# A two-layer encoder on one core: mixer tokens in column order, mixer B's products 160 wide, and all its heads turned by VectorE and GpSimd

## The chip, the cores and the metric

The kernel runs on one core of a Trainium2 chip. The metric is the device time of one execution in microseconds, as the median of several runs. The engines are TensorE (PE in the profile, its weight loads PEld), VectorE (DVE), ScalarE (ACT), GpSimd (POOL) and SyncE (SP), which issues the DMAs. Each engine works through its own list of instructions in order and waits on semaphores for what it needs from the others.

## The reference

An encoder of two layers over 256 tokens with 2048 features, all in float32. Each layer has a sub-layer of two mixers side by side and a feed-forward sub-layer; the shift, scale and gate of each come from one linear map of `c` ("ada"). Cut to what matters here:

```python
h = rmsnorm(x, norm_mix[l]) * (1.0 + sc_a) + sh_a
qa, ka, va, qb, kb, vb, ga, gb = split_cols(h @ w_in[l])
ya = window_attention(qa, ka, va, sink_a[l]) @ w_proj_a[l]        # 8 heads, |i-j| <= 128
yb = neighbourhood_attention(qb, kb, vb, rel_bias_b[l]) @ w_proj_b[l]  # 8 heads
merged = jax.nn.sigmoid(ga) * ya + jax.nn.sigmoid(gb) * yb
x = x + gt_a * (merged @ w_out[l])
h = rmsnorm(x, norm_ffn[l]) * (1.0 + sc_m) + sh_m
u = depthwise_conv(h @ w_up[l], conv_w[l], conv_b[l])
g, v = jnp.split(u, 2, axis=-1)
x = x + gt_m * ((jax.nn.silu(g) * v) @ w_down[l])
```

The 256 tokens of mixer B are a grid of 4 rows by 64 columns, token = row * 64 + column. A token attends to all 4 rows (`NA_KH` is 8, clamped to 4) and to a window of 16 columns around its own, with a learned bias by the offset; all other scores are -1e30 before the softmax.

## The kernel before

Activations lie with features on partitions and 256 tokens along a row. All weights are streamed once, in the order of use, as units of 16 blocks of 128x128: a DMA of 1 MB on SP into a tile `w` (four buffers, shared with the ada tiles `aw`), then in two halves ScalarE casts the block to a rounded fp32r high part and VectorE subtracts for the low part (`hl`, lines 326 and 327). TensorE makes three products for each block, high times high, high times low and low times high (lines 343 to 345 with 256 columns; lines 406 to 408 with 512 columns, where the weights move and the tokens are stationary: that is how q, k, v come out with tokens on partitions). The ada map is a row reduction on VectorE (line 233, 2.35 us for each of 189 tiles of 1 MB).

Everything else is fitted between the units. `Stream.tick` runs after each unit and lets background jobs go on; one of them is `attention()`, a generator in which each live head takes one step at a time: its start (for mixer B with the load of its bias into `p`, line 880), scores and softmax, for some heads the turn of the probabilities, their split into high and low parts (`pT`), and the product with v (`po`, line 689). A scheduler in the framework then settles the order on each engine; on SP it is the order of issue. SP's DMAs take eight landing semaphores in turn (DMAHW0 to DMAHW7), and a DMA waits until the one that had its semaphore before has landed.

The pieces that the change touches:

- `normed` (line 494) writes the modulated norm `ht` on VectorE (line 497), from which ScalarE and VectorE make the high and low parts of h, for both sub-layers (`w` is 0 for the mixers).
- `small(l)` loads the tables: maskA (128x512), cs (the rotary table, 128x64), gains, rg, sink and cw, one DMA each (line 178).
- `attend` makes a head's scores as two products of 256 keys for 128 queries each. In layer 0 these are plain float32 (two passes on TensorE for one product), in layer 1 three fp32r products each (`SCORES_3`). The reduction at line 654 adds mask or bias and takes the maximum, ScalarE makes the exponentials and the scaling (lines 662 and 670).
- The turn: in layer 0, four transposes of 128x128 on TensorE into `tp` (line 681). In layer 1, VectorE transposes blocks of 32x32 (line 304) and GpSimd puts the blocks in their places with 16 copies of 32x128 (line 298). `MOVED = [(0,0), (8,8)]` says how many heads of mixers A and B in each layer are turned in this second way. ScalarE and VectorE then write `pT` (lines 418 and 421) and TensorE makes po with six products of 256 columns.
- In the gates and the merge, mixer A's branch `ya` is multiplied by its gate, mixer B's by `gb`, and `merge` adds both on VectorE (line 1014) and splits the sum for `w_out`.

Of the kernel before, what the change touches and what calls it, by code (L numbers as in the profile page):

```python
# [30 lines left out]
BLOCK = 32  # L31

# [57 lines left out]
MOVED = [(0,0), (8,8)]  # L90
# [51 lines left out]
def encoder(ctx: ExitStack, tc: tile.TileContext, a: dict, out: bass.AP):  # L142
# [45 lines left out]
    sp = pool("s", 1)  # L188

# [118 lines left out]

    def unit_steps(l, u, by_halves=False):
# [181 lines left out]
    def normed(l, w, h, rbs):  # L491

        mod, amod = mods[l], amods[l]
        for kc in range(KC):
            t = ev.tile([P, S], F32, name="ht", tag="z")
            sh = mod[:, 3 * w * KC + kc : 3 * w * KC + kc + 1]
            nc.vector.scalar_tensor_tensor(
                out=t[:], in0=x[:, kc], scalar=amod[:, w, kc : kc + 1], in1=rbs[:], op0=ALU.mult, op1=ALU.mult
# [147 lines left out]
    def attend(q, k, v, p, mask, scale, sink, o, rows=None):  # L646

        sc = ax.tile([P, 2, S], F32, name="sc", tag="ax")
        for t in range(2):
            for i, j in by(q):  # L650
                nc.tensor.matmul(sc[:, t], q[i][:, t * P : (t + 1) * P], k[j], start=i + j == 0, stop=(i, j) == by(q)[-1])  # L651
        m = sm.tile([P, 2], F32, name="m", tag="m")
        for t in range(2):
            nc.vector.tensor_tensor_reduce(
                out=p[:, t], in0=sc[:, t], in1=mask[:, t], scale=scale, scalar=-3.0e38 if sink is None else sink,
                op0=ALU.add, op1=ALU.max, accum_out=m[:, t : t + 1],
            )
# [3 lines left out]
        for t in range(2):  # L661
            nc.scalar.activation(out=p[:, t], in_=p[:, t], func=AF.Exp, bias=nm[:, t : t + 1], accum_out=den[:, t : t + 1])
# [6 lines left out]
        for t in range(2):  # L669
            nc.scalar.activation(out=p[:, t], in_=p[:, t], func=AF.Copy, scale=ri[:, t : t + 1])  # L670
        yield
        if rows is not None:
            turned_blocks(p[:], rows(), 2)
            for _ in range(STEPS[sink is None]):
                yield
            tp = p
        else:
# [5 lines left out]
        split(pT, tp[:], held=rows is not None)  # L683
# [124 lines left out]
    for l in range(L):  # L808
# [17 lines left out]
        if l:  # L826


            def bare_gate(mo):
                def evac(ps):  # L830
                    z, sh = bare.level(ps, 0.5)
                    half_tanh(ya[:, mo], z[:], bias=sh[:, :1])
# [17 lines left out]
        def head_a(i):  # L850
# [18 lines left out]
            def rows():  # L869
# [3 lines left out]
                q, k, v, p, tables[0], SCALE, sink[:, i : i + 1], lambda: oA[i], rows if i < MOVED[l][0] else None  # L873
            )

        def head_b(hb):
# [3 lines left out]
            nc.sync.dma_start(p[:], a["bias"][l, hb])  # L880
# [323 lines left out]
```

## Time and profile before

| | us |
|---|---|
| median of 3 runs | 2653.98 |
| lowest, highest | 2653.20, 2656.04 |
| the profiled execution's own time | 2661.45 |
| its span in the trace | 2659.6 |
| TensorE busy | 2643.3 |
| VectorE busy | 2121.0 |
| ScalarE busy | 1408.9 |
| GpSimd busy | 228.2 |

A share of busy time is a mean over stages with different limits, so the page's totals only say where to look. What counts is, stage by stage, which engine is full and how long before its use each operand is there. The 40 slices of the page show TensorE at 90% or more in each slice, so a stall of TensorE is lost time wherever it falls, and work of another engine costs only where TensorE has to wait for it. Matmuls overlap in the records, so a product's price is the distance from one start to the next in the timeline, or the length of a stretch over the count, not its own duration.

The trace has the granted TensorE clock at 1.00 throughout. The DMA queues moved 700.42 MB at a mean of 263 GB/s, 371 GB/s in the first slice.

### The profile page before, as it was taken

The page shows a single profiled execution, that of the slowest core. Times are in us where ns is not written, and L with a number is a line of the kernel's source. Part 1 is how long each engine was busy: PE and PEld are TensorE (multiplying, and loading weights), DVE is VectorE, ACT ScalarE, POOL GpSimd, SP SyncE. Part 2 cuts the span into 40 slices and gives each one's busy share as a digit, 9 for nine tenths or more (in the row PEclk, how much of TensorE's full clock was granted, in tenths as well). Part 3 has the DMA queues.
Part 4 walks back from the last instruction along what each step waited for, and adds up shares of the span by engine and source line. Part 5 has one row for each costly group of instructions (what it writes and reads, how often), then busy time and mean ns, then how long its engine had stood idle before and what let it go on. Part 6 is the DMA issues. An engine that isn't in the chain of part 4 may idle for free.

```text
span 2659.6 us, 51014 instructions
## 1 busy us (share of the span) xinstructions
PE 2643.3 (99%) x21164; PEld 2557.9 (96%) x21164; DVE 2121.0 (80%) x2979; ACT 1408.9 (53%) x2280; POOL 228.2 (9%) x345
## 2 busy tenths in 40 slices
PE   9999999999999999999999999999999999999999
PEld 7888899999999999999998889999999999999999
DVE  8898998997987888788886778868888866655664
ACT  5445865456643555355554666654565445544553
POOL 0001100000000000000002558520000000000000
PEclk9999999999999999999999999999999999999999
DMA  9987779885777777877766666666747765555554
GB/s 371 349 329 292 267 294 356 316 339 184 295 272 289 284 287 285 306 296 285 283 221 253 249 234 232 253 258 257 283 178 287 297 252 191 192 196 194 196 191 143
DMA packets 102042, 700.42 MB, mean 263 GB/s; under 512 B 12721, under 2 KB 15025, under 8 KB 17969
## 3 DMA queue, kind: packets, MB, share of 16 engines
q1 hardware_dynamic: 101810, 697.17, 70.8%
q8 instruction: 165, 2.70, 0.4%
q14 instruction: 67, 0.55, 0.1%
HBM read 695.03 MB, written 2.10 MB: 262 GB/s over the span
## 4 chain that ended last, share of the span: by engine, by line
PE 86%; DMA 5%; DVE 5%; issue 2%; ACT 1%; POOL 0%; SPq 0%; DVEq 0%; ACTq 0%
PE ps L343 24%; PE ps L345 24%; PE ps L344 24%; DMA aw<-in_aw 4%; PE ps_t L408 4%; PE ps_t L407 4%; PE ps_t L406 4%; DVE hl L327 2%; DVE aw L233 1%; PE sc L651 1%; ACT hl L326 1%; PE po L689 1%; DMA w<-in_ws 1%; DVE u L1049 0%; POOL qrs L472 0%
## 5 line engine op out<-in xcount | busy, mean ns | idle before, releaser
L327 DVE TENSOR_TENSOR hl<-w,hl 128x1024 fp32r<-128x1024 f32 x928 | 1129.8, 1224 | 298.0 <-ACT hl L326 294.7
L326 ACT CAST hl<-w 128x1024 fp32r<-128x1024 f32 x928 | 969.8, 1049 | 719.7 <-PE ps L345 501.4
L343 PE MATMUL ps<-h,hl 128*128 128x256 f32 x3328 | 922.4, 277 | 1.3 <-DVE ya L970 0.6
L344 PE MATMUL ps<-h,hl 128*128 128x256 f32 x3328 | 919.6, 276 | 0.0
L345 PE MATMUL ps<-h,hl 128*128 128x256 f32 x3328 | 919.6, 277 | 0.0
L343 PEld LDWEIGHTS ps<-h,hl 128*128 128x128 f32 x3328 | 624.7, 188 | 2.4 <-DVE ya L970 0.8
L344 PEld LDWEIGHTS ps<-h,hl 128*128 128x128 f32 x3328 | 625.3, 188 | 0.4 <-DVE h L501 0.2
L345 PEld LDWEIGHTS ps<-h,hl 128*128 128x128 f32 x3328 | 624.4, 188 | 0.0
L233 DVE CUSTOM_DVE_ANT_0 aw<-aw,cact,ab 128x2048 f32<-128x2048 f32 x189 | 443.8, 2349 | 92.5 <-DMA aw<-in_aw 91.7
L406 PE MATMUL ps_t<-hl,h 128*128 128x512 f32 x576 | 223.0, 392 | 2.7 <-ACT h L500 2.0
L407 PE MATMUL ps_t<-hl,h 128*128 128x512 f32 x576 | 225.0, 391 | 0.3
L408 PE MATMUL ps_t<-hl,h 128*128 128x512 f32 x576 | 224.3, 390 | 0.0
L1049 DVE SCALAR_TENSOR_TENSOR u<-ps,cw,u 128x255 f32<-128x255 f32 x304 | 146.0, 480 | 62.0 <-ACT u L1047 58.1
L1047 ACT ACTIVATE u<-ps,cw 128x256 f32<-128x256 f32 x152 | 85.7, 564 | 155.4 <-PE ps L345 155.2
L343 PE MATMUL ps<-act_o,hl 128*128 128x256 f32 x512 | 142.0, 278 | 2.7 <-DVE u L1049 2.6
L345 PE MATMUL ps<-act_o,hl 128*128 128x256 f32 x512 | 142.1, 278 | 1.3 <-DVE hl L327 1.3
L344 PE MATMUL ps<-act_o,hl 128*128 128x256 f32 x512 | 142.0, 277 | 0.0
L345 PE MATMUL ps<-merged,hl 128*128 128x256 f32 x512 | 141.5, 277 | 0.0
L344 PE MATMUL ps<-merged,hl 128*128 128x256 f32 x512 | 141.5, 276 | 0.0
L343 PE MATMUL ps<-merged,hl 128*128 128x256 f32 x512 | 141.5, 277 | 0.0
L406 PEld LDWEIGHTS ps_t<-hl,h 128*128 128x128 f32 x576 | 107.9, 188 | 26.1 <-ACT h L500 3.0
L407 PEld LDWEIGHTS ps_t<-hl,h 128*128 128x128 f32 x576 | 108.1, 188 | 23.9 <-DVE hl L327 1.9
(244 smaller groups left out, 4800.3 us busy)
## 6 DMA issues: line engine op xcount, KB each, us to landing
w<-in_ws SPq DMA_DIRECT2D x463, 1024.0 KB, 4.9
aw<-in_aw SPq DMA_DIRECT2D x189, 1024.0 KB, 6.3
p<-in_bias SPq DMA_DIRECT2D x16, 256.0 KB, 4.5
x<-in_xT SPq DMA_DIRECT2D x4, 512.0 KB, 5.5
aw_o<-in_aw SPq DMA_DIRECT2D x2, 1024.0 KB, 12.4
out<-x SPq DMA_DIRECT2D x16, 128.0 KB, 3.2
w<-in_ws SPq DMA_DIRECT2D x2, 512.0 KB, 11.8
aw_b<-in_aw SPq DMA_DIRECT2D x1, 1024.0 KB, 18.1
```

Of the source, the lines that this page charges most:

```text
L233: nc.vector.tensor_tensor_reduce(out=raw[:], in0=raw[:], in1=cact[:], scale=1.0, scalar=ab[:, i : i + 1], op0=ALU.mult, op1=ALU.add, accum ...
L326: nc.scalar.copy(hl[:, 0], r)
L327: nc.vector.tensor_tensor(out=hl[:, 1], in0=r, in1=hl[:, 0].bitcast(F32), op=ALU.subtract)
L343: nc.tensor.matmul(out, hi, act[0], start=first, stop=False)
L344: nc.tensor.matmul(ps[:, :S], hi, act[1], start=False, stop=False)
L345: nc.tensor.matmul(out, lo, act[0], start=False, stop=last)
L406: nc.tensor.matmul(ps[:], xh, hi, start=kc == kcs[0], stop=False)
L407: nc.tensor.matmul(ps[:], xh, lo, start=False, stop=False)
L408: nc.tensor.matmul(ps[:], xl, hi, start=False, stop=kc == kcs[-1])
L651: nc.tensor.matmul(sc[:, t], q[i][:, t * P : (t + 1) * P], k[j], start=i + j == 0, stop=(i, j) == by(q)[-1])
L1047: nc.scalar.activation(out=u, in_=ps, func=AF.Identity, scale=w[:, 1:2], bias=w[:, 3:4])
L1049: nc.vector.scalar_tensor_tensor(out=u[:, to], in0=ps[:, of], scalar=w[:, j : j + 1], in1=u[:, to], op0=ALU.mult, op1=ALU.add)
```

## The change

The tokens of the mixers (both of them) are put in column-by-column order: token = column * 4 + row. In that order the 16 columns that a token sees are close together, and each half of 128 queries needs only 160 keys (`NEAR` = 128 + 32). x and the feed-forward keep the order row by row. In detail:

- `normed` for the mixers writes `ht` with a step between elements (tokens in the new order). The gates that layer 1 takes from the bare activations are written so too. `merge` writes its sum back in row order, with a step, into a second tile.
- Tables and biases that are indexed by token are loaded in the new order by `load_tokens`, four DMAs of 64 partitions for each: 4 for maskA (through a tile `seen` and two GpSimd copies that reorder the keys), 8 for cs, 4 for each of the 16 biases.
- In mixer B the scores, the softmax and po work on 160 keys or queries for each half. po has seven products (160, 64, 96 and four times 160 columns), since the first product of the second half splits where it meets columns not yet written.
- All heads of mixer B in both layers (`WINDOWS_FROM = [0, 0]`) are turned by VectorE's transpose of two times 160 columns (`turned_near`) and 12 GpSimd copies, ten of 32x2x32 and two of 32x32. The probabilities stand in the q and k slots of the head in `packB`, and the bias tile `p` takes the turned blocks. So layer 0's heads of mixer B have one step more than before. Mixer A is turned as before.

```diff
-MOVED = [(0,0), (8,8)]
+MOVED = [0, 8]
+WINDOWS_FROM = [0, 0]
...
+    def load_tokens(dst, src):
+        rows = src.rearrange("(q w c) h f -> w q c h f", q=GRID_H // 2, w=2)
+        for w in range(2):
+            for q in range(GRID_H // 2):
+                nc.sync.dma_start(dst[q::2, w], rows[w, q])
...
+    def turned_near(p, turned):
+        nc.vector.transpose(out=near(turned), in_=near(p))
+        for a in range(P // BLOCK):
+            for d in (-1, 0, 1):
+                b = (a + d) % 4
+                dst, src = p[b * BLOCK : (b + 1) * BLOCK], turned[a * BLOCK : (a + 1) * BLOCK]
+                if a + d == b:
+                    to, of = (sheared(x, i * BLOCK, P, BLOCK) for x, i in ((dst, a), (src, b)))
+                else:
+                    t = int(d < 0)
+                    to, of = (x[:, i, P - BLOCK * i : P + BLOCK * (1 - i)] for x, i in ((dst, 1 - t), (src, t)))
+                nc.gpsimd.tensor_copy(out=to, in_=of)
...
+    def split_near(dst, src, held):
+        high, low = near(dst[:, 0]), near(dst[:, 1])
+        copied = nc.scalar.copy(high, near(src))
+        if held:
+            tc.keep_in_program_order(copied)
+        nc.vector.tensor_tensor(out=low, in0=near(src), in1=high.bitcast(F32), op=ALU.subtract)
...
+            to, of, roots = (t[:], x[:, kc], rbs[:]) if w else (columns_by_row(t[:]), by_rows(x[:, kc]), by_rows(rbs[:]))
             nc.vector.scalar_tensor_tensor(
-                out=t[:], in0=x[:, kc], scalar=amod[:, w, kc : kc + 1], in1=rbs[:], op0=ALU.mult, op1=ALU.mult
+                out=to, in0=of, scalar=amod[:, w, kc : kc + 1], in1=roots, op0=ALU.mult, op1=ALU.mult
...
-                nc.tensor.matmul(sc[:, t], q[i][:, t * P : (t + 1) * P], k[j], start=i + j == 0, stop=(i, j) == by(q)[-1])
+                nc.tensor.matmul(
+                    sc[:, t, :n], q[i][:, t * P : (t + 1) * P], k[j][:, part(t)], start=i + j == 0, stop=(i, j) == by(q)[-1]
+                )
...
-                nc.tensor.matmul(po[:, :S], v[i][:, b], pT[:, j, b], start=i + j + b == 0, stop=i + b == 2)
+                fresh = window and b == 1 and i + j == 0
+                for c in (slice(S - n, n), slice(n, S)) if fresh else (part(b),):
+                    nc.tensor.matmul(po[:, c], v[i][:, b], pT[:, j, b, c], start=i + j + b == 0, stop=i + b == 2)
...
-            tables.extend((load(a["maskA"], [P, 2, S], "maskA"), load(a["cs"], [P, 2, 2, HALF], "cs")))
+            seen = at.tile([P, 2, S], F32, name="seen", tag="p")
+            load_tokens(seen[:], a["maskA"])
+            mask = const.tile([P, 2, S], F32, name="maskA")
+            for t in range(2):
+                nc.gpsimd.tensor_copy(out=by_columns(mask[:, t]), in_=rows_by_column(seen[:, t]))
+            cs = const.tile([P, 2, 2, HALF], F32, name="cs")
+            for f in range(2):
+                load_tokens(cs[:, f], a["cs"][:, f])
+            tables.extend((mask, cs))
...
-            nc.sync.dma_start(p[:], a["bias"][l, hb])
+            load_tokens(p[:], a["bias"][l, hb])
...
-                nc.vector.tensor_tensor(out=z[:], in0=z[:], in1=ya[:, mo], op=ALU.add)
-                split(merged[mo], z[:], 0.5)
+                both = ev.tile([P, S], F32, name="m2", tag="z")
+                nc.vector.tensor_tensor(
+                    out=rows_by_column(both[:]), in0=by_columns(z[:]), in1=by_columns(ya[:, mo]), op=ALU.add
+                )
+                split(merged[mo], both[:], 0.5)
```

The order of DMAs on SP at unit 15 of layer 0, where the tables are loaded, first before (`w_15` and `w_16` are weight units, `aw_17` an ada tile; in brackets the semaphores that a DMA waits for):

```order
L315 DMA w_15_974<-in_ws 128x2048 [waits DVE_49]
L178 DMA maskA<-in_maskA 128x512
L178 DMA cs<-in_cs 128x64 [waits DMAHW2_49]
L178 DMA gains_992<-in_gains 128x4
L178 DMA rg_994<-in_rg 128x64 [waits DMAHW4_49]
L178 DMA sink_996<-in_sink 128x8 [waits DMAHW5_49]
L178 DMA cw_998<-in_cw 128x352 [waits DMAHW6_49]
L232 DMA aw_17_1033<-in_aw 128x2048 [waits DMAHW7_49,DVE_49]
L315 DMA w_16_1037<-in_ws 128x2048 [waits DMAHW0_49,DVE_49]
```

and with the change from the first piece of cs on (four pieces of `seen` stand between `w_15` and it):

```order
L223 DMA cs<-in_cs 64x1x16 [waits DMAHW5_49]
L223 DMA cs<-in_cs 64x1x16 [waits DMAHW6_49]
L223 DMA cs<-in_cs 64x1x16 [waits DMAHW7_49]
L223 DMA cs<-in_cs 64x1x16 [waits DMAHW0_49]
L223 DMA cs<-in_cs 64x1x16 [waits DMAHW1_49]
L223 DMA cs<-in_cs 64x1x16 [waits DMAHW2_49]
L223 DMA cs<-in_cs 64x1x16 [waits DMAHW3_49]
L223 DMA cs<-in_cs 64x1x16 [waits DMAHW4_49]
L181 DMA gains_1005<-in_gains 128x4 [waits DMAHW5_49]
...
L181 DMA cw_1011<-in_cw 128x352 [waits DMAHW0_49]
L267 DMA aw_17_1046<-in_aw 128x2048 [waits DMAHW1_49,DVE_49]
L364 DMA w_16_1050<-in_ws 128x2048 [waits DMAHW2_49,DVE_49]
```

The fourth piece of cs takes the semaphore that `w_15` had, `cw` that of the fourth piece, `aw_17` and `w_16` those of the fifth and sixth.

The order on TensorE around head B0 of layer 0, before (`tp` are B0's transposes, `sc` the scores of the next head, B1, and `po` with `vB_0` is B0's):

```order
L681 MATMUL tp<-ident,p 128x128
L651 MATMUL sc<-packB_0_224 128x256
L681 MATMUL tp<-ident,p 128x128 x3
L651 MATMUL sc<-packB_0_224 128x256
L344 MATMUL ps_54_8_0_3451<-oA_4_2735,hl_53_1_3423 128x256
L345 MATMUL ps_54_8_0_3451<-oA_4_2735,hl_53_1_3423 128x256
L343 MATMUL ps_54_8_0_3451<-oA_4_2735,hl_53_1_3423 128x256
L344 MATMUL ps_54_8_0_3451<-oA_4_2735,hl_53_1_3423 128x256
L689 MATMUL po<-pT,vB_0_3210 128x256 x2
```

and now, ahead of B0's `po` (its seven products, the last four in one row):

```order
L392 MATMUL ps_54_8_0_3476<-oA_7_2953,hl_53_1_3448 128x256
L393 MATMUL ps_54_8_0_3476<-oA_7_2953,hl_53_1_3448 128x256
L394 MATMUL ps_54_8_0_3476<-oA_7_2953,hl_53_1_3448 128x256
L782 MATMUL po<-pT,vB_0_3326 128x160
L782 MATMUL po<-pT,vB_0_3326 128x64
L782 MATMUL po<-pT,vB_0_3326 128x96
L782 MATMUL po<-pT,vB_0_3326 128x160 x4
L715 MATMUL sc<-packB_0_224 128x160 x2
```

In the new order TensorE has 61 products with weights, 6 of the `po` of a mixer-A head, 8 transposes of q and k and 4 score products between B0's second score product and B0's `po`; the four transposes of B0's probabilities are gone.

On VectorE, from the first half of unit 54 on, before (line 421 with `tp` is the low part of B0's `pT`):

```order
L327 TENSOR_TENSOR hl_54_0_3517<-w_54_3515,hl_54_0_3517 128x1024
L233 ISA aw_45_3636,mod_172<-aw_45_3636,cact,ab_173 128x2048
L233 ISA mod_172 128x1
L421 TENSOR_TENSOR pT<-tp,pT 128x512
L654 ISA p,m<-sc,p 128x256
```

and now (line 346 is B0's turn, line 483 the low part of its `pT`):

```order
L376 TENSOR_TENSOR hl_54_0_3555<-w_54_3553,hl_54_0_3555 128x1024
L346 STREAM_TRANSPOSE p<-packB_0_224 128x2x160
L491 SCALAR_TENSOR_TENSOR ya_222<-ya_222,ps_53_16_0_3442 128x256
L725 ISA packB_0_224,m<-sc,p 128x160
L725 ISA m 128x1
L725 ISA packB_0_224,m<-sc,p 128x160
L725 ISA m 128x1
L376 TENSOR_TENSOR hl_54_1_3558<-w_54_3553,hl_54_1_3558 128x1024
L730 TENSOR_SCALAR nm<-m 128x2
L483 TENSOR_TENSOR pT<-packB_0_224,pT 128x2x160
L491 SCALAR_TENSOR_TENSOR ya_222<-ya_222,ps_54_8_0_3476 128x256
L376 TENSOR_TENSOR hl_55_0_3618<-w_55_3616,hl_55_0_3618 128x1024
```

Between the turn and the low part there are now the reductions of head B1 and the second half of unit 54; the first half of unit 55 stands behind the low part. The 12 GpSimd copies of B0 lie between lines 346 and 483.

More of the change, by code (lines that the diff above doesn't have):

```diff
@@ L31 @@
 BLOCK = 32
+GRID_H = S // GRID_W
+NEAR = P + BLOCK
 QKV_GROUPS = [1024, 0, 512, 2560, 3584, 1536, 3072, 4096, 2048]
@@ L661, in attend @@
         for t in range(2):
-            nc.scalar.activation(out=p[:, t], in_=p[:, t], func=AF.Exp, bias=nm[:, t : t + 1], accum_out=den[:, t : t + 1])
+            e = p[:, t, part(t)]
+            nc.scalar.activation(out=e, in_=e, func=AF.Exp, bias=nm[:, t : t + 1], accum_out=den[:, t : t + 1])
         if sink is not None:
@@ L682, in attend @@
         pT = at.tile([P, 2, 2, S], F32R, name="pT", tag="pT", bufs=1)
-        split(pT, tp[:], held=rows is not None)
+        if window:
+            split_near(pT, tp, rows is not None)
+        else:
+            split(pT, tp[:], held=rows is not None)
         v = v()
@@ L872, in head_a @@
             yield from attend(
-                q, k, v, p, tables[0], SCALE, sink[:, i : i + 1], lambda: oA[i], rows if i < MOVED[l][0] else None
+                q, k, v, p[:], tables[0], SCALE, sink[:, i : i + 1], lambda: oA[i], rows if i < MOVED[l] else None
             )
```

52 lines of the change are left out of this document (45 added, 7 removed).

## The prediction

> **What bounds the kernel now.** First the page's shares of busy time and the engines of the chain that ended last:
>
> ```profile
> span 2659.6 us, 51014 instructions
> ...
> PE 2643.3 (99%) x21164; PEld 2557.9 (96%) x21164; DVE 2121.0 (80%) x2979; ACT 1408.9 (53%) x2280; POOL 228.2 (9%) x345
> ...
> PE 86%; DMA 5%; DVE 5%; issue 2%; ACT 1%; POOL 0%; SPq 0%; DVEq 0%; ACTq 0%
> ```
>
> TensorE is busy for 2643.3 of 2659.6 us. It bounds the kernel, and only 16.3 us of idle time can be won anywhere. So the change can gain by fewer or cheaper TensorE instructions, and it can lose wherever it makes TensorE wait. The profiled execution took 2661.45 us by its own clock (1.85 us lie around the span), 0.28% over the median of 2653.98; the sum below is made against the span and its difference put on the median.
>
> Next the stretches that the change touches. The columns are the stretch, its length, then busy time and count of PE, PEld, DVE, ACT and POOL, the clock, the DMA share and GB/s:
>
> ```profile
> 17.00:85.00 68.00, 64.38 (x366) 53.96 (x365) 60.87 (x69) 38.03 (x57) 0.00 (x0) 1.00 0.97 379
> 340.00:380.00 40.00, 40.00 (x318) 38.27 (x317) 38.45 (x80) 25.20 (x53) 0.00 (x0) 1.00 0.79 292
> 475.00:560.00 85.00, 85.00 (x748) 85.00 (x747) 79.11 (x127) 43.47 (x70) 0.00 (x0) 1.00 0.82 309
> 1800.00:1850.00 50.00, 50.00 (x440) 50.00 (x439) 47.71 (x84) 27.00 (x45) 0.00 (x0) 1.00 0.68 257
> 2400.00:2450.00 50.00, 50.00 (x442) 50.00 (x441) 26.11 (x28) 19.84 (x20) 0.00 (x0) 1.00 0.55 193
> ```
>
> The start (17 to 85 us) is the only one where TensorE idles (3.6 us), with the DMA at 0.97 and VectorE busy for 60.87 of 68. Around layer 0's mixer-B heads (340 to 380) VectorE is full to 38.45 of 40, in the merges of layer 0 (475 to 560) to 79.11 of 85 and in those of layer 1 (1800 to 1850) to 47.71 of 50: there VectorE work has little room. The last row is plain weight products: 50/442 = 0.113 us for one fp32r product of 256 columns.
>
> **TensorE's own work (term a).** The timeline of TensorE at head B0 of layer 0, and its weight loads where products have one column:
>
> ```profile
> 341.63 0.60 PE L651 MATMUL sc<-packB 128*128 128x256 f32 x2
> 342.06 0.49 PE L681 MATMUL tp<-ident,p 128*128 128x128 f32 x3
> 342.39 0.60 PE L651 MATMUL sc<-packB 128*128 128x256 f32 x2
> ```
>
> ```profile
> 1358.76 0.53 PEld L461 LDWEIGHTS ssf<-mean,sq 128*128 128x128 f32 x4
> 1359.21 0.19 PEld L344 LDWEIGHTS ps<-bare_a,hl 128*128 128x128 f32 x1
> ```
>
> From start to start, one plain F32 score product is two passes in 0.43 us (0.215 each), and a transpose is 0.33/3 = 0.11. Four weight loads of one-column products take 0.45 us: 0.11 each with next to nothing to stream, so the load is a floor of 0.11 however narrow the product is. By that:
> - Layer 0's scores: 8 heads x 2 products x 2 passes; a pass of 160 columns by its width is 0.134 instead of 0.215: 32 x 0.08 = -2.6.
> - Layer 0's transposes of mixer B go: 32 x 0.11 = -3.5.
> - po of all 16 heads: seven products at the floor instead of six of 0.113: 16 x 0.09 = +1.5.
> - Layer 1's 48 score products: 0.113 to 0.11, -0.2.
>
> Sum of a: -4.8. No row has an fp32r product between 1 and 256 columns wide, so its bounds are the two nearest rates. By width alone (0.113 x 160/256 = 0.07; po 960 columns instead of 1536) po gives -4.1 and layer 1's scores -2.0, in all -12.2. At the F32 rate (0.43 us per 256, so 0.27 per 160) po gives +15.0 and the scores +7.5, in all +16.4. I take the floor, since the one-column rows lie on it.
>
> **The queue of loads (term b).** SP's own timeline where the small tables are loaded, and the landing times of the cs table and of the weights between 84 and 130 us:
>
> ```profile
> 96.14 0.33 SPq L315 DMA_DIRECT2D w<-in_ws  x1
> 96.52 0.43 SPq L178 DMA_DIRECT2D maskA<-in_maskA  x1
> 96.99 0.43 SPq L178 DMA_DIRECT2D cs<-in_cs  x1
> ...
> 99.08 0.45 SPq L178 DMA_DIRECT2D cw<-in_cw  x1
> 100.74 0.33 SPq L232 DMA_DIRECT2D aw<-in_aw  x1
> 103.04 0.33 SPq L315 DMA_DIRECT2D w<-in_ws  x1
> ```
>
> ```profile
> DMA to landing us min/median/max: 5.8/5.8/5.8
> DMA to landing us min/median/max: 5.3/7.0/7.9
> ```
>
> and of all aw tiles, the last number, from the page:
>
> ```profile
> aw<-in_aw SPq DMA_DIRECT2D x189, 1024.0 KB, 6.3
> ```
>
> Each DMA takes the next of eight landing semaphores and waits until the DMA eight before it has landed. Today two tables, four small ones, then aw 17 and w 16 follow the w of 96.14. The change puts 12 DMAs where two were. The eighth behind that w, the fourth piece of cs, now waits for its landing (96.14 + 7.0, about 103.2). The four small tables wait for the first four pieces of cs; the last of them, cw, for the piece issued at 103.2: 103.2 + 5.8 = 109.0. Then come aw 17 at about 109.3 instead of 100.74 and w 16 at about 109.7 instead of 103.04. What hangs on these two:
>
> ```profile
> 110.54 2.00 ACT L326 CAST hl<-w 128x1024 fp32r<-128x1024 f32 x2 [3.60 <-DMA w<-in_ws]
> ```
>
> ```profile
> 111.01 2.35 DVE L233 CUSTOM_DVE_ANT_0 aw<-aw,cact,ab 128x2048 f32<-128x2048 f32 x1
> 115.06 2.35 DVE L327 TENSOR_TENSOR hl<-w,hl 128x1024 fp32r<-128x1024 f32 x2
> ```
>
> ```profile
> 116.58 0.62 PE L406 MATMUL ps_t<-hl,h 128*128 128x512 f32 x2
> ```
>
> ScalarE already waited 3.6 us for w 16; the first low half is there after half of the pair, at 115.06 + 1.2 = 116.3, and TensorE uses it at 116.58: 0.3 us of slack. VectorE works in order, so aw 17's pass of 2.35 us holds up everything behind it. With the 6.3 us of aw's landing it begins at 109.3 + 6.3 = 115.6 instead of 111.0, and the low half is 4.6 to 5 us late. Lowest 0 (the small pieces land at once), highest 6.5 (the whole delay of w 16). I take +4.8, and it is lost for good, since TensorE has no idle time behind it to catch up.
>
> **Stepped outputs (term c).** Four groups of VectorE by shape (count, then busy us and mean ns), and the count of ht between 17 and 85 us:
>
> ```profile
> L497 DVE SCALAR_TENSOR_TENSOR ht<-x,amod,rbs 128x256 f32<-128x256 f32 x64 | 28.8, 477 | 0.5
> L1014 DVE TENSOR_TENSOR m<-m,ya 128x256 f32<-128x256 f32 x32 | 13.5, 421 | 0.3
> L421 DVE TENSOR_TENSOR pT<-p,pT 128x512 fp32r<-128x512 f32 x16 | 11.9, 741 | 0.1
> L304 DVE STREAM_TRANSPOSE packB<-p 128x512 f32<-128x512 f32 x8 | 5.7, 709 | 5.1 <-ACT p L670 5.1
> ```
>
> ```profile
> 17.00:85.00 68.00, 3.39 (x7) 1.00 0.97 379
> ```
>
> The first sub-layer's ht, and the merges, now write with a step. The trace has no stepped output. At nothing extra the cost is 0; at a second time slot for each element it is 256 x (741-421)/256 = 0.32 us, so 7 x 0.32 = 2.2 at the start. VectorE is 90% busy there and TensorE waits, so I take the middle, +1.0. In the merges 16 x 0.32 = 5.1 us stand against 85 - 79.1 = 5.9 us of free VectorE in layer 0 and 2.3 in layer 1: 0 to 2.8, taken as 0.5 in term e.
>
> [...]
>
> **Head B0 of layer 0 (term d).** Before, TensorE turned its probabilities; now VectorE and 12 GpSimd copies do. ScalarE, VectorE and GpSimd rows:
>
> ```profile
> 349.26 0.90 ACT L670 ACTIVATE p<-p,ri 128x256 f32<-128x256 f32 x2
> ```
>
> ```profile
> 349.38 1.23 DVE L327 TENSOR_TENSOR hl<-w,hl 128x1024 fp32r<-128x1024 f32 x1
> ```
>
> ```profile
> L298 POOL COPY p<-packB 32x128 f32<-32x128 f32 x128 | 77.8, 608 | 35.5 <-DVE packB L304 17.7 <-issue 11.4 <-POOL p L298 1.3
> L298 POOL COPY p<-spare 32x128 f32<-32x128 f32 x16 | 6.5, 406 | 11.0 <-DVE spare L304 10.3
> ```
>
> The second score product ends at 342.99 and the probabilities are scaled at 350.16. The order puts the turn behind the low half that ends at 350.6. Then: the turn, 320/512 of 0.709 = 0.44; 12 copies of half the size, between 12 x 0.2 = 2.4 (half of 0.406) and 12 x 0.608 = 7.3, taken as 4.5 (the smaller row, a little less for the size); the cast, about 0.37 (0.90/2 for 256 columns, so not more than 0.56 for 320); the low part, 0.46. po can start 13.4 us after the scores (11.3 to 16.2). By the new order TensorE has 61 products and 6 of po of the head before (67 x 0.113 = 7.6), 8 transposes (0.9) and 4 score products of 8 passes (1.1) before that po: 9.6, at most 10.2 where a narrow pass keeps its 0.215. So TensorE waits between 1.1 and 6.6 us; by the taken values 3.5. VectorE stands still too: the low part of pT follows closely behind the turn, and the next weights' low half (hl_55) stands behind it, so nothing makes the wait good. The later heads have longer spacings; layer 1's heads were turned by GpSimd before, with 16 larger copies, and lie off the path.
>
> **The rest (term e).** Three more SP issues of 0.43 us per head (the row of maskA) and bias loads that wait for GpSimd's copies, since the mask tile is now the turn's scratch; the next weight load stands behind them on SP. With the DMA at 0.79 there I take 0.5, and 0.5 for the merges: +1.0 (0 to 4).
>
> **Sum.** -4.8 + 4.8 + 1.0 + 3.5 + 1.0 = +5.5. Span 2659.6 to 2665.1; median 2653.98 + 5.5 = 2659.5. The forecast's own range, from the bounds of b to e: 2652 to 2665.
>
> **Rivals.**
> 1. Small pieces cost by their size, on every engine. For it: a GpSimd copy of 128 elements was 0.406 in one group, and a transpose of 128 columns takes half of an F32 pass of 256. Against it: the 0.11 us of one-column loads, and cs, a small table, taking 5.8 us to land. It decides from where a piece of cs lands in under 1 us. Then a = -12.2, b = 0, c = 0, d = 1.4, e = 0.5: -10.3, 2643.7, faster.
> 2. The tables' turn doesn't reach TensorE: pieces of cs land in about 2 us, or aw 17 finds VectorE with other work to put ahead. b falls away: +0.7, 2654.7. For it: the DMA is idle for a while if SP waits, so what is issued then lands sooner. Against it: 0.3 us of slack.
> 3. Stepped operations cost twice their whole time, and VectorE becomes the bound: ht 7 x 0.48 = 3.3; merges 16 x 0.42 = 6.7, less 5.9 and less 2.3, so 0.8 + 4.4. Instead of 1.0 and 0.5 that is 8.5: +12.5, 2666.5. For it: 47.71 of 50. Against it: no row at all.
> 4. Narrow fp32r products fall to the F32 rate: a = +16.4 instead of -4.8: +26.7, 2680.7. For it: F32 and fp32r already differ by 0.43 to 0.113 at one width. Against it: a one-column fp32r product needs one weight load, where F32 makes two passes.
>
> That the change doesn't do what it says is excluded by the order: layer 0's transposes of mixer B are gone and the widths are 160.
>
> **How the numbers follow.** Forecast 0.48, rival 1 0.12, rival 2 0.15, rival 3 0.15, rival 4 0.08, something else 0.02. About 0.2% (5.3 us: 2648.7 to 2659.3) is what a measurement tells from no change. The forecast lies at the upper edge of that: I give 0.27 of its 0.48 to slower, 0.19 to same and 0.02 to faster. Slower: 0.27 + 0.15 + 0.08 = 0.50; same: 0.19 + 0.15 + half of the rest = 0.35; faster: 0.12 + 0.02 + half of the rest = 0.15. The range 2646 to 2669 leaves out rival 4 and most of rival 1.
>
> **What would show it.** a: the pitch of po's products of 160 columns, 0.11 (0.07 for rival 1, 0.27 for rival 4). b: the SP row of aw 17 near 109 us, and a gap of TensorE of 4 to 5 us near 117. c: ht's mean above 477 ns and the merge's above 421. d: a gap of TensorE ahead of B0's po near 353 us, with GpSimd's 12 copies before it. I am wrong if TensorE shows no gap at either place, or if the narrow products are far from 0.11.

## The result, and the profile after

The changed kernel takes 2716.64 us (median of 5 runs, 2716.37 to 2717.4) against 2654.02 us: 62.6 us more, a ratio of 1.0234 with a 95% interval of 1.0219 to 1.0249. It is slower, as forecast, but by eleven times the 5.5 us of the sum, and far outside the range.

The page of the changed kernel, with the span, the busy times and the engines of the chain that ended last:

```profile
span 2714.6 us, 51142 instructions
...
PE 2660.6 (98%) x21148; PEld 2572.1 (95%) x21148; DVE 2128.0 (78%) x2987; ACT 1403.2 (52%) x2280; POOL 250.0 (9%) x411
...
PE 73%; DVE 4%; issue 3%; POOL 2%; DMA 2%; ACT 1%; SPq 0%; POOLq 0%; DVEq 0%; ACTq 0%
```

TensorE has less to do, and yet its busy time is 17.3 us longer than before. Its share of the chain falls from 86 to 73%, and GpSimd's rises from 0 to 2%.

Where the time goes is best seen by following the same weights through both traces. The start of the last product on a half of a weight unit, found by counting the products in order:

| layer, unit, half | before, us | after, us | behind by |
|---|---|---|---|
| 0, 15, second | 116.3 | 119.6 | 3.2 |
| 0, 16, second | 121.8 | 130.9 | 9.1 |
| 0, 57, first | 379.6 | 388.4 | 8.7 |
| 0, 63, second | 419.3 | 451.8 | 32.5 |
| 1, 50, second | 1652.0 | 1680.8 | 28.8 |
| 1, 63, second | 1730.3 | 1785.0 | 54.7 |
| 1, 231, second | 2656.0 | 2711.1 | 55.1 |

Three places make nearly all of it: 5.9 us at unit 16 of layer 0, 24 us in the mixer-B heads of layer 0, 26 us in those of layer 1. The windows of the changed kernel over these places (stretch, length, then busy time and count of PE, PEld, DVE, ACT, POOL; clock, DMA share, GB/s) show them, and (third row) the merges of layer 0 behind its heads:

```profile
95.00:130.00 35.00, 31.05 (x167) 26.35 (x166) 28.56 (x39) 12.99 (x18) 2.57 (x2) 0.95 0.76 285
340.00:460.00 120.00, 101.64 (x774) 98.91 (x773) 88.63 (x160) 54.04 (x119) 40.54 (x84) 0.90 0.63 242
475.00:600.00 125.00, 124.33 (x1092) 124.13 (x1091) 117.04 (x168) 60.83 (x100) 5.94 (x7) 1.00 0.87 327
1675.00:1790.00 115.00, 98.80 (x786) 97.81 (x785) 72.88 (x136) 50.57 (x102) 34.91 (x72) 0.91 0.57 211
```

In the head stages TensorE idles for 18 and 16 us, while VectorE and ScalarE are less busy than before and the DMA share falls to 0.63 and 0.57. No engine is full there. Something holds up the loads.

SP's timeline in layer 0's heads shows what (start, duration, DMA, count):

```profile
392.12 2.40 SPq L223 DMA_DIRECT2D p<-in_bias  x4
394.56 0.58 SPq L267 DMA_DIRECT2D aw<-in_aw  x1
395.26 0.36 SPq L364 DMA_DIRECT2D w<-in_ws  x1
395.72 0.38 SPq L267 DMA_DIRECT2D aw<-in_aw  x1
396.88 0.33 SPq L364 DMA_DIRECT2D w<-in_ws  x1
410.89 2.40 SPq L223 DMA_DIRECT2D p<-in_bias  x4
413.33 0.58 SPq L267 DMA_DIRECT2D aw<-in_aw  x1
414.01 0.38 SPq L364 DMA_DIRECT2D w<-in_ws  x1
```

and GpSimd's timeline beside it, the 12 copies of two heads:

```profile
386.12 5.98 POOL L356 COPY packB<-p 32x32 f32<-32x32 f32 x12 [5.29 <-PE sc L715]
...
403.84 7.02 POOL L356 COPY packB<-p 32x32 f32<-32x32 f32 x12 [11.75 <-issue]
```

The copies end at 386.12 + 5.98 = 392.10 and at 403.84 + 7.02 = 410.86; the bias loads are issued at 392.12 and 410.89. Each bias load waits for the copies, because the tile that it fills, `p`, is the scratch of the turn of the head before the last. From 397 to 410.9 SP issues nothing, and the ada and weight loads stand behind the bias in its list. ScalarE's cast of the weights issued at 414.01 then waits for them:

```profile
421.01 1.99 ACT L375 CAST hl<-w 128x1024 fp32r<-128x1024 f32 x2 [5.46 <-DMA w<-in_ws]
```

In layer 1 the late load is most often the ada tile. Waits of VectorE from 1675 to 1790 us (waited for: us in total, times, longest):

```profile
DVE aw L268 <- DMA aw<-in_aw: 26.8, 5, 8.5
DVE packB L725 <- DMA p<-in_bias: 6.2, 2, 5.5
```

The low half of the weights stands behind that ada pass in VectorE's list, and TensorE waits for the low half: four times in this window, for 14.9 us.

SP's own waits for the copies, from 330 to 470 us and from 1640 to 1790 us (us in total, times, longest):

```profile
SPq L223 <- POOL packB L356: 33.1, 6, 7.4
...
SPq L223 <- POOL packB L356: 42.2, 6, 10.6
```

In layer 1 the kernel before held the same tile longer still: 16 copies write back into it, and then the low part of pT is read from it. All of SP's waits for that, from 1640 to 1790 us:

```profile
SPq L880 <- DVE pT L421: 5.1, 7, 1.2
```

So the hold of the tile is not what is new in layer 1. The bias load now stands so far ahead in SP's list that SP comes to it long before the copies end. Why the framework's order puts it there isn't shown.

The wait isn't the whole price. TensorE's timeline at the longest gap in layer 0:

```profile
437.63 0.28 PE L393 MATMUL ps<-h,hl 128*128 128x256 f32 x1
437.75 0.28 PE L394 MATMUL ps<-h,hl 128*128 128x256 f32 x1
443.86 0.58 PE L392 MATMUL ps<-h,hl 128*128 128x256 f32 x1 [5.82 <-ACT hl L375]
...
445.71 0.41 PE L393 MATMUL ps<-h,hl 128*128 128x256 f32 x1
445.92 0.41 PE L394 MATMUL ps<-h,hl 128*128 128x256 f32 x1
```

Before the gap one product follows the other after 0.12 us, behind it after 0.21, until about 448.3. The granted clock (the third number from the right) was at half there and whole again behind it:

```profile
443.86:448.25 4.39, 3.92 (x16) 3.63 (x17) 4.39 (x4) 2.30 (x5) 2.61 (x2) 0.50 1.02 429
448.26:452.20 3.94, 3.94 (x36) 3.94 (x36) 3.90 (x6) 1.58 (x3) 3.77 (x5) 1.00 1.01 401
```

That is why TensorE's busy time grew and the clock in the windows reads 0.90 and 0.91. Over the whole span the distances of over 1 us from one product's start to the next sum to 46.9 us against 10.2 before, 37 us more. And TensorE was busy for 38.6 us at a clock of 0.50, against none before, which costs it half of that, 19 us. Less the 4.8 us of work that the change saves by the prediction's term a, that is 51 of the span's 55.0. (The median moved by 62.6: the profiled execution of the kernel before took 7.5 us more than its median, most of it in waits for loads between 750 and 850 us that the profile of the column order alone, below, doesn't have.)

### The profile page after: what moved, and what is told of

The parts are those of the page before. It is cut to its first block, busy times and chain, and to the rows that moved or that the text cites. A ratio compares the mean times of both kernels' runs of the same rounds, so it can differ in the third digit from the quotient of the medians.

```text
span 2714.6 us, 51142 instructions
## 1 busy us (share of the span) xinstructions
PE 2660.6 (98%) x21148; PEld 2572.1 (95%) x21148; DVE 2128.0 (78%) x2987; ACT 1403.2 (52%) x2280; POOL 250.0 (9%) x411
## 4 chain that ended last, share of the span: by engine, by line
PE 73%; DVE 4%; issue 3%; POOL 2%; DMA 2%; ACT 1%; SPq 0%; POOLq 0%; DVEq 0%; ACTq 0%
PE ps L392 22%; PE ps L394 22%; PE ps L393 22%; PE ps_t L457 2%; PE ps_t L456 2%; PE ps_t L455 2%; DVE hl L376 2%; POOL packB L356 1%; DMA aw<-in_aw 1%; DVE aw L268 1%; DMA w<-in_ws 0%; POOL packB L333 0%; POOL p L333 0%; PE po L782 0%; ACT hl L375 0%
## 5 line engine op out<-in xcount | busy, mean ns | idle before, releaser
L392 PE MATMUL ps<-h,hl 128*128 128x256 f32 x3328 | 927.4, 279 | 10.2 <-ACT hl L375 7.8
```

What stands on the lines that cost most here:

```text
L392: nc.tensor.matmul(out, hi, act[0], start=first, stop=False)
```

## The experiments

Theory T: the bias load waits for GpSimd's copies, and SP's list is blocked behind it. Rival R1: the turn's own chain (VectorE, 12 copies, cast) is what TensorE waits for. Rival R2: the four DMAs for each bias are too many for SP. All times are medians; each run has its own runs of the kernel before beside it.

**A scratch of its own for the turn.**

```diff
-                turned_near(p, mask)
+                turned_near(p, rows())
...
+            def rows():
+                return packs[1 + (hb - 1) // 4][:, (hb - 1) % 4 :: 8] if hb else paired(F32, f"spare{l}_b")
```

> The change, with one edit: the turn of a mixer-B head uses the pair of slots of the head before it as its scratch (a spare pair for head 0), so the bias tile p is free after the reductions and not only after the 12 GpSimd copies. Theory T (the bias of the head after next waits on SP for those copies, and the weight and ada loads stand behind it): the gaps of TensorE of 1 us and more between 360 and 450 us and between 1680 and 1785 us go, and with them the half-rate products after them; about 46 of the 62.6 us come back, 2671 us (2662 to 2685). Rival R1 (the turn's own chain of VectorE, 12 copies and the held cast is what TensorE waits for): 2708 to 2717. Rival R2 (four DMAs for each bias, 2.4 us of SP time, are the loss): 2700 to 2717.

2678.85 us (before: 2655.46). 37.8 of the 62.6 us are back. Windows of this run over both head stages, and its waits of TensorE from 340 to 440 us:

```profile
340.00:430.00 90.00, 79.01 (x631) 77.62 (x630) 73.99 (x134) 43.83 (x93) 14.14 (x51) 0.95 0.70 257
...
1660.00:1750.00 90.00, 90.00 (x786) 90.00 (x785) 69.83 (x125) 49.96 (x98) 26.55 (x64) 1.00 0.70 248
```

```profile
PE po L782 <- ACT pT L480: 10.8, 4, 3.4
```

Layer 1's loss is gone: TensorE is busy for 90.00 of 90 us, though the same copies run. By the starts of the weight units, 25 us are back in layer 1 and 13 in layer 0. Layer 0 still has four gaps, at the heads B0 to B3, and they end on `pT`, not on a load: that is R1's chain, which takes over in layer 0 once the loads are in time. T holds for the larger part. Layer 0 is the weaker evidence, because the framework's order moved its heads as well: B0's copies begin at 395.2 us here and at 359.9 in the changed kernel.

**One DMA for each bias.**

```diff
-            load_tokens(p[:], a["bias"][l, hb])
+            nc.sync.dma_start(p[:], a["bias"][l, hb])
...
-    bias = bias.reshape(L, HB, 2, P, S).transpose(0, 1, 3, 2, 4)
+    bias = bias[:, :, perm].reshape(L, HB, 2, P, S).transpose(0, 1, 3, 2, 4)
```

> The change, with one edit: the bias is laid out by the host with its queries in the new order, so each head has one DMA instead of four; the wait for GpSimd's copies stays. T: SP is blocked as long as before, but what stands behind the bias is issued some 2 us earlier for each head: 5 to 20 us come back, 2697 to 2712. R2: nearly all of the 48 us of the two head stages come back, 2665 to 2675. R1: under 5 us, 2712 to 2717.

2707.76 us: 8.9 back, in T's bounds. SP's pauses ahead of the bias loads stay as long (51.8 us in layer 0's heads, 59.8 in layer 1's). The 2.4 us of SP time for four issues lie behind the wait and are added to it; they aren't its cause. R2 falls.

**One DMA for each table.**

```diff
-            seen = at.tile([P, 2, S], F32, name="seen", tag="p")
-            load_tokens(seen[:], a["maskA"])
...
-            tables.extend((mask, cs))
+            tables.extend((load(a["maskA"], [P, 2, S], "maskA"), load(a["cs"], [P, 2, 2, HALF], "cs")))
...
+    maskA = maskA[perm][:, perm].reshape(2, P, S).transpose(1, 0, 2)
```

> The change, with one edit: maskA and cs are laid out by the host in the new order and loaded by one DMA each. All theories: only the gap near 120 us (3.9 us, then half-rate products) goes, the two head stages stay as they are: 5 to 9 us come back, 2708 to 2712. If the tables' pieces were not its cause: 2715 to 2718.

2706.58 us: 10.1 back, a little more than expected. At unit 16 itself it is 5.8; by the units' starts, most of the rest lies in the start of the kernel (2 us) and in layer 0's merges (3 us). The window in which the changed kernel had TensorE busy for 31.05 us at a clock of 0.95:

```profile
95.00:130.00 35.00, 35.00 (x185) 30.07 (x184) 32.68 (x46) 16.41 (x21) 0.00 (x0) 1.00 0.95 346
```

The gap is gone and the clock is whole.

**The old turn in layer 0 of the kernel before.**

```diff
-MOVED = [(0,0), (8,8)]
+MOVED = [(0,8), (8,8)]
```

> The kernel before, with one edit: the eight mixer-B heads of layer 0 are turned in the old way too, by VectorE's transpose of 512 columns and 16 GpSimd copies of 32x128 (MOVED (0,8) for layer 0); token order, widths and the single bias DMA stay. T: the bias tile is held until the copies have ended here too, and the loads behind the next bias are late in layer 0 only: slower than before by 15 to 35 us, 2669 to 2689, with gaps between 345 and 450 us and none in layer 1. R2: no loss, 2648 to 2656, since each bias is one DMA. R1: slower by 10 to 35 us as well, but the gaps end on po or pT and not on late loads.

2663.77 against 2655.46 us: 8.3 us, a ratio of 1.003 (1.002 to 1.004). Less than the lowest of T and of R1. Its waits of TensorE between 340 and 450 us:

```profile
PE po L689 <- ACT pT L418: 4.8, 1, 4.8
PE ps L345 <- DVE hl L327: 3.6, 1, 3.6
```

The larger gap is of R1's kind, the other ends on a low half. So holding the bias tile is not enough by itself. SP's timeline at its longest pause ahead of a bias load in this run:

```profile
362.32 0.33 SPq L315 DMA_DIRECT2D w<-in_ws  x1
368.56 0.33 SPq L880 DMA_DIRECT2D p<-in_bias  x1
```

That is 5.9 us, against 14.1 in the changed kernel. SP's pauses ahead of bias loads, from 330 to 470 us (layer 0) and from 1630 to 1790 us (layer 1):

| | layer 0: sum, longest, us | layer 1: sum, longest, us |
|---|---|---|
| kernel before | 15.2, 3.8 | 5.4, 1.2 |
| old turn in layer 0 | 29.6, 5.9 | 5.4, 1.2 |
| scratch of its own | 27.1, 7.5 | 9.7, 2.2 |
| changed kernel | 55.4, 14.1 | 58.3, 13.6 |

In the three runs with short pauses in layer 1, TensorE has no gap of over 1 us in its heads. This fits a cost that goes with the length of the pause, not with the wait as such; the length was not varied by itself.

**The bias loads on GpSimd's queue.**

```diff
-            load_tokens(p[:], a["bias"][l, hb])
+            load_tokens(p[:], a["bias"][l, hb], nc.gpsimd)
```

> The change, with one edit: the four DMAs of each bias are issued by GpSimd instead of SP. They still wait for the copies of the head before the last, but the weight and ada loads are no longer behind them. T (a blocked SP queue is the loss): layer 1's gaps between 1680 and 1785 us go and layer 0 keeps at most the gaps that end on po: 2675 to 2692. Rival (the late bias itself holds up the heads, whatever queue it stands on): 2700 to 2717.

2686.53 us (before: 2654.13), in T's bounds: the same wait for the same copies costs 30 us less when it blocks no weights. By the units' starts, the head stages lose 2 us in layer 0 and 9.6 in layer 1, against 23 and 26 in the changed kernel. One new gap of 6.2 us comes near 1647 us. GpSimd's timeline and VectorE's there:

```profile
1640.81 6.49 POOL L333 COPY packB<-qn 32x256 f32<-32x256 f32 x13
1647.25 2.22 POOL L223 DMA_DIRECT2D p<-in_bias  x4
```

```profile
1650.07 0.43 DVE L725 CUSTOM_DVE_ANT_1 packB<-sc,p 128x160 f32<-128x160 f32 x1 [8.25 <-DMA p<-in_bias]
```

Here the bias itself is late, behind GpSimd's copies of q, and VectorE waits 8.25 us for it: the queue that is blocked has changed, not the kind of loss.

**Layer 0 turned by TensorE again.** The 160-wide work stays.

```diff
-WINDOWS_FROM = [0, 0]
+WINDOWS_FROM = [8, 0]
...
-        elif window:
-            tp = ax.tile([P, 2, S], F32, name="tp", tag="ax")
...
```

> The change, with one part undone: the mixer-B heads of layer 0 are turned by TensorE (four transposes of 128x128 each, the halves outside the 160 keys zeroed by a GpSimd memset); everything else as in the change. T: layer 0's gaps between 360 and 450 us go (the step from 9 to 32 us behind the kernel before), 32 transposes of 0.11 us come back (3.5 us), layer 1's gaps stay: 2690 to 2702. If only the interplay of both layers or the tables made the loss in layer 0: over 2705.

2694.41 us: 22.2 back, from layer 0 alone. Windows over both head stages:

```profile
340.00:430.00 90.00, 88.53 (x745) 86.70 (x745) 80.41 (x149) 50.22 (x113) 1.81 (x7) 1.00 0.77 290
1650.00:1760.00 110.00, 93.19 (x717) 92.03 (x716) 68.01 (x126) 46.76 (x95) 28.46 (x64) 0.89 0.56 203
```

Layer 0 is whole but for 1.5 us; layer 1 has its loss still. So layer 1's loss needs none in layer 0.

**Three edits together:** own scratch, tables and biases in one DMA each (the diffs above).

> The change with three edits: scratch of its own for the turn, tables in one DMA each, biases in one DMA each. By T and the single runs: 2678.9 of the run with its own scratch, less 10 for the tables and 2 to 6 for the biases: 2660 to 2668, with gaps left only where po of layer 0 waits for the turn (four of some 3 us). If the single gains overlap: 2668 to 2676.

2679.57 us. Not one of the 12 to 16 us came. The gap at unit 16 is gone, but the time was given back in layer 0's merges. Windows from 470 to 580 us of the run with its own scratch, then of this one:

```profile
470.00:580.00 110.00, 109.34 (x960) 109.13 (x960) 101.88 (x148) 53.02 (x86) 6.95 (x10) 1.00 0.88 327
```

```profile
470.00:580.00 110.00, 105.92 (x897) 105.29 (x896) 97.98 (x145) 50.63 (x84) 3.61 (x4) 0.97 0.81 303
```

TensorE now idles for 4.1 us there and loses clock (0.97 instead of 1.00). That the stall at unit 16 had given VectorE and the loads time to get ahead is my reading; no run shows it. The expectation's range for overlapping gains (2668 to 2676) is missed too.

**Layer 0 by TensorE, with the three edits,** and the bias's keys laid out in the new order too.

```diff
-                add = rows_by_column(add)[:, first : first + n // GRID_H]
+                add = add[:, part(t)]
```

> As the run with three edits, and layer 0's mixer-B heads turned by TensorE, and the keys of the bias laid out by the host in the new order too (so the reductions read without a step). By T no gap of 1 us is left that the kernel before does not have, and TensorE's own work is below it by 2.6 us (scores of layer 0) less 1 us (seven products of po): 2650 to 2656 against 2655 before. If the stepped writes of ht and merges cost TensorE time: 2657 to 2663.

2665.55 us against 2654.13, a ratio of 1.0041 (1.0028 to 1.0054). That is over the range by T alone and over the one with stepped writes too. Two gaps, of 2.1 and 1.6 us near 538 us, are ones that the kernel before doesn't have. The next runs divide the 11 us that remain.

**No steps at all.** This run leaves out the reordering of tokens; ht, bare gates and merges are written straight.

```diff
-                    out=rows_by_column(both[:]), in0=by_columns(z[:]), in1=by_columns(ya[:, mo]), op=ALU.add
+                    out=both[:], in0=z[:], in1=ya[:, mo], op=ALU.add
```

> The run of layer 0 by TensorE with the other edits (2665.6), with the stepped writes of ht, the bare gates and the merge written straight instead; it leaves out the reordering of tokens between grid and column order, and all work keeps its size. Theory S (0.2 us more for each stepped VectorE write makes VectorE the bound in the merges, and TensorE waits there between 500 and 600 us): 2651 to 2657. Rival (what is left of the loss comes from late biases, SP's issues or the turn in layer 1): 2662 to 2667.

2662.63 us, in the rival's range: steps cost some 3 us of the 11, and the single times of both runs overlap (2659.7 to 2665.6 here, 2663.0 to 2666.7 there). My theory S falls for the rest. Waits of VectorE from 400 to 500 us in this run, and the same row of the kernel before:

```profile
DVE aw L268 <- DMA aw<-in_aw: 17.9, 13, 2.6
```

```profile
DVE aw L233 <- DMA aw<-in_aw: 2.2, 3, 1.3
```

The ada tiles are late by small amounts behind the heads. By the units' starts, TensorE then loses 5.1 us from unit 63 to unit 100, where the merges are. That VectorE carries the late ada work into them is my reading.

**TensorE reads the steps.** Only the merge is straight; the products with w_out read `merged` in steps of 16 bytes.

```diff
+            out = to(ps[:, :S])
+            nc.tensor.matmul(out, hi, of(act[0]), start=first, stop=False)
...
+                st.features(ms, [out_evac(mo) for mo in mos], sums.first if end else None, order=(columns_by_row, by_rows))
```

> The same run, with only the merge written straight; TensorE reads merged with a step in the products with w_out, so the reordering stays complete. If TensorE reads steps of 16 bytes at full rate, by S: 2655 to 2661, w_out's products at 0.113 us and the gaps near 540 us gone. If a stepped moving operand costs TensorE: 1536 products at 0.05 us more or worse, over 2700.

2845.73 us, 180 more. A stretch of nothing but these products:

```profile
580.00:620.00 40.00, 40.00 (x173) 35.67 (x172) 18.90 (x25) 9.56 (x14) 0.00 (x0) 1.00 0.50 184
```

40/173 = 0.231 us for one product against 0.113: half rate, at a full clock. 1536 x 0.118 = 181 us.

**The column order alone, in the kernel before.** Steps, and tables laid out by the host; 256 wide, old turns.

```diff
+            to, of, roots = (t[:], x[:, kc], rbs[:]) if w else (columns_by_row(t[:]), by_rows(x[:, kc]), by_rows(rbs[:]))
...
+                    out=rows_by_column(both[:]), in0=by_columns(z[:]), in1=by_columns(ya[:, mo]), op=ALU.add
```

> The kernel before with the column order alone: tokens of the mixers in the new order by stepped writes of ht, bare gates and merges, tables and biases laid out by the host with one DMA each as before; widths of 256, turns and products as before. S: slower than before by 4 to 12 us, 2658 to 2667, with gaps between 480 and 570 us. If VectorE hides the steps: 2653 to 2657.

2656.48 against 2654.3 us, a ratio of 1.0008 (0.9999 to 1.0018): 2.2 us, in an interval that includes no change, and in agreement with the 3 us above. The stepped writes add 13.1 us to VectorE's work (64 ht of 576 ns in the mean instead of 477, 32 merges of 633 instead of 421), so VectorE hides nearly all of it.

**160 wide, but probabilities in the bias tile.**

```diff
-        if window and rows is None:
+        if window:
             nc.gpsimd.memset(sheared(p, NEAR, -NEAR, S - NEAR), 0.0)
...
-                b[:, i : 9 + i : 8], p[:], 1.0, None, lambda: oB_of(hb), rows if hb >= WINDOWS_FROM[l] else None,
+                p[:], p[:], 1.0, None, lambda: oB_of(hb), rows if hb >= WINDOWS_FROM[l] else None,
```

> The kernel with the column order alone (2656.5), with the products, the softmax and the split of mixer B 160 wide as well; the probabilities stay in the bias tile, whose columns outside the 160 keys GpSimd sets to zero; turns as in the kernel before (TensorE in layer 0, VectorE and 16 copies in layer 1), tables and biases laid out by the host with one DMA each. If the place of the probabilities, and with it the point at which the bias tile is free and its load stands on SP, made the 9 us between 2656.5 and 2665.6: 2652 to 2657 here. If the narrow work itself (more and shorter instructions, seven products of po) made them: 2661 to 2666.

2672.57 us, outside both ranges. In layer 1 the memset stands among the copies in GpSimd's list and waits for the bias (the 16 memsets wait 81.0 us for biases, 72.1 of them from 340 to 470 us, which leaves 8.9 for layer 1), so there the run brought a wait of its own: 5.4 us by the units' starts in that head stage. In layer 0 there are no copies for it to hold up, and 9.7 us are lost from unit 63 to unit 100, against 7.3 in the run with layer 0 by TensorE and 1.2 with the column order alone. So, by one trace, layer 0's loss stays with the probabilities in the bias tile, and their place is not what makes it. For layer 1 the run decides nothing.

**Layer 0 as before, layer 1 as mended.**

```diff
-        window = sink is None
+        window = sink is None and rows is not None
```

> The kernel with the column order alone (2656.5) for layer 0, with mixer B of layer 0 as in the kernel before (256 wide, turned by TensorE, probabilities in the bias tile); layer 1's mixer B as in the run with layer 0 by TensorE (160 wide, VectorE and 12 copies, scratch of its own). If the narrow work in layer 0 made the 9 us between 2656.5 and 2665.6 (late ada tiles between 400 and 500 us, VectorE full in the merges behind): 2654 to 2659, no gap near 540 us. If layer 1's new turn made them: 2662 to 2667.

2659.53 against 2654.24 us, just over the range for layer 0. By the medians, layer 0's narrow work makes 6 of the 9 us between 2656.5 and 2665.6, and layer 1's new turn 3. The traces bear out the first part (2.1 us are lost from unit 63 to 100 of layer 0, against 7.3) and half of the second: in layer 1, 1.6 us are lost up to unit 100, against none with the column order alone. How the narrow work in layer 0 makes the ada tiles late wasn't settled. No version was faster than the kernel before.

## Why the prediction was wrong, step by step

**Bound.** Right: TensorE bounds the kernel, and what made it wait decided.

**Term a (TensorE's work).** Right. TensorE's timeline in layer 1 has the seven products of po, then six score products:

```profile
1724.53 0.90 PE L782 MATMUL po<-pT,vB 128*128 128x160 f32 x7
1725.27 0.83 PE L715 MATMUL sc<-kB,qB 128*128 128x160 f32 x6
1725.94 0.32 PE L392 MATMUL ps<-oA,hl 128*128 128x256 f32 x1
```

0.74/7 = 0.106 and 0.67/6 = 0.112 us: the floor of 0.11, which excludes rivals 1 and 4. For fp32r only this run shows it: the one-column rows from which the step read the floor, and rival 4 its "one-column fp32r product", are plain F32 (line 461, two products as four records). A plain F32 pass of layer 0's scores took 0.136 us for 160 columns, against 0.134 in the sum. The 4.8 us of saved work are drowned by 19 us lost to the halved clock, for which the sum had no term.

**Term b (the queue of loads).** Mechanism and place right, size a little low. SP's timeline:

```profile
99.40 0.33 SPq L364 DMA_DIRECT2D w<-in_ws  x1
...
113.11 0.36 SPq L267 DMA_DIRECT2D aw<-in_aw  x1
113.58 0.37 SPq L364 DMA_DIRECT2D w<-in_ws  x1
```

From that w to aw 17 it took 13.7 us; the step said 13.2. TensorE waited 3.9 us near 120, and then ran at half rate (clock 0.50 from 124.0 to 127.4): 5.9 us at this unit, against 4.8. The run without the pieces loses nothing there. Rival 2 is excluded, although the pieces of cs did land after 2.1 us (median).

**Term c (steps).** Right. VectorE's groups:

```profile
L555 DVE SCALAR_TENSOR_TENSOR ht<-x,amod,rbs 128x256 f32<-128x256 f32 x64 | 34.6, 579 | 2.1 <-ACT rbs L540 1.7
...
L1116 DVE TENSOR_TENSOR m<-m,ya 128x256 f32<-128x256 f32 x32 | 20.3, 635 | 0.2
```

Half of the ht are stepped, so a stepped one takes 2 x 579 - 477 = 681 ns, 0.20 us more; the merge 0.21. The two runs on steps give 2 and 3 us for the kernel, against 1.0 in term c and 0.5 in term e. Rival 3, a doubling, is excluded.

**Term d (head B0).** Its size was right (a gap of 2.9 us at 361.7, taken as 3.5), and B0's copies took 4.2 us, taken as 4.5. Its limit was not: "The later heads have longer spacings". With the loads in time, the heads B0 to B3 each wait for their turn, 10.8 us in all, 8.1 of it behind B0. That layer 1's heads "lie off the path" held for the turn itself (90.00 of 90 us busy with a scratch of its own), but not for the loads behind it.

**Term e (the rest) is the step that failed.** "Three more SP issues of 0.43 us per head (the row of maskA) and bias loads that wait for GpSimd's copies, since the mask tile is now the turn's scratch; the next weight load stands behind them on SP. With the DMA at 0.79 there I take 0.5". The mechanism is named there, and priced at 0.5 us, by the room on the DMA. What counts is how long SP's list is blocked against how early the loads behind the wait are needed. The list was blocked until the copies ended, 14 us at the longest, and before the change the low half of a weight unit was ready at most 8.0 us ahead of its first use in layer 0's heads and 7.4 in layer 1's. By the run that takes the wait away it cost 37.8 us, in both layers and with the halved clock behind most of the gaps. None of the rivals had it.

**The copies** of the other heads were longer than B0's. The mean of a copy of 32x64 elements is 0.521 us, against 0.608 for 32x128 before: half the size, hardly less time. The 12 of a head took from 3.2 to 12.8 us, 6.5 in the mean, and term e, where their length mattered, had no term for it.

**The range.** With a at -4.8, the bounds of b to e add up to 3.7 us less to 14.5 us more, a median of 2650 to 2668.5, somewhat wider than the 2652 to 2665 that the sum gives. It changes nothing here: no bound had a blocked list or a halved clock.

## What to carry to other kernels

When a change moves the release of a tile from one engine to another, look where the load into that tile now stands in the in-order DMA list. For each such load, count how long the list is blocked and set that against the slack of every load behind it, not against the mean DMA share. A scratch tile that was also a load's destination brought this wait here, 37.8 us of it. And price a stall of TensorE with what follows it: in the changed kernel the halved clock cost some 19 us on top of 37 us of gaps.

## What the runs showed of the hardware that was not expected

- Behind most of the longer gaps of the changed kernel the granted clock is at half for some microseconds: 0.21 us for a product instead of 0.12 from 443.9 to 448.3 us. Ten such stretches, of 3.4 or 6.8 us each, make 47.8 us in which the clock was 0.50. All six gaps of 3.9 to 6.1 us have one, behind them or beginning in them, and so have shorter ones, down to 1.6 us near 1750 us. A gap of 2.2 us near 624 us has none, and the clock stayed at 1.00 behind one of 2.9 us near 780 us in the kernel before. By what rule the clock falls isn't shown.
- A moving operand of TensorE that steps 16 bytes with each fp32r element took 0.231 us instead of 0.113 for 256 columns, at a clock of 1.00, in the run where the products with w_out read `merged` so: a factor of two. No run here has another step, so what other steps cost isn't shown.
- Narrow fp32r products cost what 256 columns cost (0.113 us): 0.106 in the mean for the seven of po, of 64 to 160 columns, and 0.112 for score products of 160, with a weight load for each product (21148 of both on the page). Nothing was won here by making them narrower. A plain F32 pass did fall with the width, from 0.218 us for 256 columns to 0.136 for 160 (medians from one start to the next).
